# A rotary embedding kernel: an alignment instruction ahead of VectorE's and GpSimd's work

## The chip, the cores and the metric

The kernel runs on one core of a Trainium2 chip. The metric is the device time of one execution in microseconds (us). A profile of one execution is at hand as well: every instruction of the five engines (TensorE = PE, VectorE = DVE, ScalarE = ACT, GpSimd = POOL, SyncE = SP), and every packet that the core's 16 DMA engines moved, with its start, its duration, its size and its queue.

## The reference

The input `x` has 8 batches of 2048 positions, 8 heads and 64 numbers per head, in float32 (33.5 MB); `cos` and `sin` are tables of 2048 x 32. Each head's vector is split into two halves, which are rotated:

```python
x1 = x[..., : x.shape[-1] // 2]
x2 = x[..., x.shape[-1] // 2 :]
out1 = x1 * cos - x2 * sin
out2 = x1 * sin + x2 * cos
return np.concatenate([out1, out2], axis=-1)
```

The output is as large as `x`, so at least 67 MB have to pass between HBM and the core's memory.

## The kernel before, in words

The 2048 positions are laid over 128 partitions, 16 positions each, so that a batch is a tile `xt` of 128 x 8192 float32 (4 MB). Five such buffers turn (`NBUF = 5`): SyncE's queue loads batches 0 to 4 at once (L67; batch 0 in three parts, with the cosine table behind the first of them, L69), and later a batch whenever the buffer of the batch five before it has been stored. ScalarE's queue loads the sine table first (L76) and then stores the finished batches (L74); the last batch is stored in three parts by SyncE's queue. The results are written over `xt` in place.

A batch is rotated in four pieces of 128 x 2048 (batch 0 and the last batch have two half pieces each). For most of them, kind "A" in the code, GpSimd makes `t2`, the halves of x swapped and multiplied by sin and by -sin (L122, two instructions), VectorE makes `t1`, x times cos (L129), and VectorE adds the two into `xt` (L136). In five pieces the addition goes elsewhere: kinds "B" and "C" add in TensorE through an identity matrix (L143, L144, L160, L161), and ScalarE copies the sum from PSUM into `xt` (L145, L165); in kind "C" VectorE makes the sine product too (L148) and GpSimd has no part in it.

The order on each engine is the order in which the code writes the instructions (`keep`). Ahead of the loop over batches stand the preparations. GpSimd fills the identity matrix `eye` (L80, L81), ScalarE makes the table -sin, a copy of sin in PSUM and the negated identity (L90 to L92), and VectorE copies cos to PSUM (L93). GpSimd's first product waits for the sine table and the first part of x, VectorE's copy for the cosine table.

The whole program is straight-line code: VectorE goes through 115 instructions and GpSimd through 95, waiting instructions and the barriers at both ends included. These instructions are themselves brought to the engines by DMA: the profile lists packets of the kind "instruction" on a queue of their own, q14.

Of the kernel before, what the change touches and what calls it, by code (L numbers as in the profile page):

```python
# [10 lines left out]
def kernel(  # L11
# [7 lines left out]
    nc = tc.nc  # L19
    keep = tc.keep_in_program_order  # L20
# [30 lines left out]
    eye = const_pool.tile([P, P], f32, tag="eye")  # L51
# [25 lines left out]
    for b in range(NBUF):  # L77
        load(b)

    nc.gpsimd.memset(eye, 0.0)  # L80
    nc.gpsimd.affine_select(  # L81
        out=eye,
        in_=eye,
# [140 lines left out]
```

## Time and profile before

| | |
|---|---|
| time, three runs | 163.49, 163.62, 163.76 us; median 163.62 us |
| span of the profiled execution, first to last instruction | 161.8 us |
| what the median has over that span | 1.8 us |
| VectorE busy | 140.1 us, 87% of the span |
| GpSimd busy | 138.9 us, 86% |
| TensorE busy | 49.4 us, 31% |
| moved by the DMA engines | 67.65 MB, 418 GB/s over the span |
| packets of instructions within the span | 2, 0.02 MB |

For the profiled execution the page gives the span as its own time; what lies around it is known only as the 1.8 us by which the median of the runs is longer. "Busy" counts the time in which an engine executes an instruction. The profile's picture of the span cuts it into 40 slices of 4.0 us and gives a digit per slice, the busy share in tenths; its row DMA is the mean over the 16 DMA engines. A packet's record has start, duration, size and queue, but not the DMA engine that moved it. q1 is SyncE's queue, q10 ScalarE's.

### The profile page before, as it was taken

How to read it: one execution, taken by the hardware profiler on the slowest of the kernel's cores; microseconds unless marked ns; L12 is line 12 of the kernel's file. 1: busy time of each engine (PE TensorE's matmuls, PEld its weight loads, DVE VectorE, ACT ScalarE, POOL GpSimd, SP SyncE). 2: the span in 40 equal slices, each digit the busy share in tenths (PEclk: the TensorE clock that was granted, in tenths of full speed). 3: DMA queues.
4: the chain of work that ended last, by engine and by line, in shares of the span. 5: the costliest groups of instructions: out<-in, count | busy, mean ns of one | idle time of the engine just before them, and what ended most of it. 6: DMA issues, size and time to landing. Idle time of an engine off the chain costs nothing.

```text
span 161.8 us, 459 instructions
## 1 busy us (share of the span) xinstructions
PE 49.4 (31%) x80; PEld 18.5 (11%) x80; DVE 140.1 (87%) x66; ACT 12.8 (8%) x14; POOL 138.9 (86%) x70
## 2 busy tenths in 40 slices
PE   0000000597309760978049714972000000000000
PEld 0000000142004220322023301330000000000000
DVE  0297999999999999999999999199989999899950
ACT  3300000002200220021000220022000000000000
POOL 1399997998999999992999959999899997999800
PEclk9999999999975998589957995699655555555555
DMA  5999999999999999899899999999999999999995
GB/s 158 425 454 494 413 308 446 413 470 405 462 405 462 389 502 405 389 510 397 389 510 397 389 512 397 397 502 397 397 488 413 405 478 413 405 478 409 397 419 225
DMA packets 3314, 67.65 MB, mean 418 GB/s; under 512 B 368, under 2 KB 368, under 8 KB 624
## 3 DMA queue, kind: packets, MB, share of 16 engines
q1 hardware_dynamic: 2016, 38.01, 55.5%
q10 hardware_dynamic: 1296, 29.62, 42.6%
q14 instruction: 2, 0.02, 0.0%
HBM read 34.08 MB, written 33.55 MB: 418 GB/s over the span
## 4 chain that ended last, share of the span: by engine, by line
DMA 48%; DVE 37%; POOL 9%; issue 2%; DVEq 0%; SPq 0%; POOLq 0%; ACTq 0%
DMA xt<-in_x_dram 26%; DVE t L129 18%; DMA out_dram<-xt 18%; DVE xt L136 17%; POOL t L122 9%; DMA sin_sb<-in_sin_dram 4%; DVE t L148 1%; DVEq L136 0%; SPq L67 0%; POOLq L122 0%; ACTq L74 0%
## 5 line engine op out<-in xcount | busy, mean ns | idle before, releaser
L122 POOL TENSOR_TENSOR t<-xt,sin_sb 128x1024 f32<-128x1024 f32 (+1 forms) x32 | 70.4, 2199 | 13.5 <-DMA xt<-in_x_dram 8.3
L129 DVE TENSOR_TENSOR t<-xt,cos_ps 128x2048 f32<-128x2048 f32 (+1 forms) x34 | 73.4, 2167 | 0.8
L122 POOL TENSOR_TENSOR t<-xt,nsin 128x1024 f32<-128x1024 f32 (+1 forms) x32 | 70.3, 2196 | 0.0
L136 DVE TENSOR_TENSOR xt<-t,t 128x2048 f32<-128x2048 f32 (+1 forms) x29 | 62.2, 2145 | 8.2 <-POOL t L122 5.5
L143 PE MATMUL o<-t,eye 128*128 128x512 f32 x24 | 17.0, 799 | 23.1 <-DVE t L129 19.6
L160 PE MATMUL o<-t,eye 128*128 128x512 f32 x16 | 12.0, 844 | 37.8 <-DVE t L129 35.6
L144 PE MATMUL o<-t,eye 128*128 128x512 f32 x24 | 14.9, 709 | 0.0
L145 ACT COPY xt<-o 128x1024 f32<-128x1024 f32 x6 | 6.1, 1012 | 45.7 <-PE o L144 45.7
L143 PEld LDWEIGHTS o<-t,eye 128*128 128x128 f32 x24 | 5.5, 256 | 32.5 <-issue 26.5
L160 PEld LDWEIGHTS o<-t,eye 128*128 128x128 f32 x16 | 3.7, 256 | 43.2 <-issue 39.4
L165 ACT COPY xt<-o 128x1024 f32<-128x1024 f32 x4 | 4.0, 1012 | 47.8 <-PE o L161 47.8
L93 DVE COPY cos_ps<-cos_sb 128x512 f32<-128x512 f32 x1 | 0.7, 695 | 6.9 <-DMA cos_sb<-in_cos_dram 6.9
L144 PEld LDWEIGHTS o<-t,eye 128*128 128x128 f32 x24 | 5.6, 234 | 8.2 <-issue 7.6
L161 PE MATMUL o<-t,neye 128*128 128x512 f32 x8 | 6.3, 875 | 0.2
L148 DVE TENSOR_TENSOR t<-xt,sin_ps 128x2048 f32<-128x2048 f32 x2 | 4.6, 2281 | 0.0
L161 PE MATMUL o<-t,eye 128*128 128x512 f32 x8 | 4.1, 592 | 0.0
L161 PEld LDWEIGHTS o<-t,neye 128*128 128x128 f32 x8 | 2.2, 300 | 5.3 <-issue 3.6
L161 PEld LDWEIGHTS o<-t,eye 128*128 128x128 f32 x8 | 1.5, 190 | 1.9 <-issue 1.9
L90 ACT ACT_TABLE_LOAD x1 | 1.3, 1283 | 1.2 <-PEq L208 1.2
L90 ACT ACTIVATE nsin<-sin_sb 128x512 f32<-128x512 f32 x1 | 0.6, 629 | 4.0 <-DMA sin_sb<-in_sin_dram 4.0
L91 ACT COPY sin_ps<-sin_sb 128x512 f32<-128x512 f32 x1 | 0.6, 580 | 0.0
L80 POOL MEMSET eye<- 128x128 f32 x1 | 0.2, 204 | 0.3 <-POOLq L208 0.3
(6 smaller groups left out, 1.0 us busy)
## 6 DMA issues: line engine op xcount, KB each, us to landing
xt<-in_x_dram SPq DMA_DIRECT2D x7, 4096.0 KB, 42.8
out_dram<-xt ACTq DMA_DIRECT2D x6, 4096.0 KB, 27.2
out_dram<-xt ACTq DMA_DIRECT2D x2, 2048.0 KB, 22.3
xt<-in_x_dram SPq DMA_DIRECT2D x2, 1024.0 KB, 6.7
xt<-in_x_dram SPq DMA_DIRECT2D x1, 2048.0 KB, 12.2
out_dram<-xt SPq DMA_DIRECT2D x1, 2048.0 KB, 9.9
out_dram<-xt SPq DMA_DIRECT2D x2, 1024.0 KB, 6.2
sin_sb<-in_sin_dram ACTq DMA_DIRECT2D x1, 256.0 KB, 5.7
```

What stands on the lines that cost most here:

```text
L90: keep(nc.scalar.mul(nsin, sin_sb, -1.0))
L93: keep(nc.vector.tensor_copy(cos_ps, cos_sb))
L122: nc.gpsimd.tensor_mul(out=t2u[:, :, u, :].rearrange("p (r h) d -> p r h d", h=H), in0=xu[:, :, 1 - u, :].rearrange("p (r h) d -> p r h d" ...
L129: nc.vector.tensor_mul(out=t1.rearrange("p (r k d) -> p r k d", r=nr, d=Dh), in0=xk, in1=rep(cos_ps[:, r0 : r0 + nr, :], 2 * H),)
L136: keep(nc.vector.tensor_add(out=xt, in0=t1, in1=t2))
L143: nc.tensor.matmul(oc, eye, t1[:, cs], start=True, stop=False)
L144: nc.tensor.matmul(oc, eye, t2[:, cs], start=False, stop=True)
L145: keep(nc.scalar.copy(xt[:, 2 * j * C : 2 * (j + 1) * C], o))
L148: nc.vector.tensor_mul(out=t2.rearrange("p (r k d) -> p r k d", r=nr, d=Dh), in0=xk, in1=rep(sin_ps[:, r0 : r0 + nr, :], 2 * H),)
L160: nc.tensor.matmul(oc, eye, t1u[:, gs, u, :], start=True, stop=False)
L161: nc.tensor.matmul(oc, eye if u else neye, t2u[:, gs, 1 - u, :], start=False, stop=True)
L165: nc.scalar.copy(xu[:, :, u, :], o.rearrange("p (g d) -> p g d", d=Dh))
```

## The change

Behind the loads of the first five batches, each of the two engines gets one alignment instruction: first VectorE, then GpSimd. It makes the loader place the engine's next instruction at a multiple of 256 instructions in that engine's code. The slots that are skipped are filled up, and `max_nops=0` says that the engine doesn't run through the filling but branches over it. On VectorE the next instruction is the copy of the cosine table, and on GpSimd the clearing of `eye`. The clearing is now also kept in program order, behind the alignment.

```diff
     for b in range(NBUF):
         load(b)
 
-    nc.gpsimd.memset(eye, 0.0)
+    for eng in (nc.vector, nc.gpsimd):
+        keep(eng.addr_align(256, max_nops=0))
+    keep(nc.gpsimd.memset(eye, 0.0))
     nc.gpsimd.affine_select(
         out=eye,
         in_=eye,
```

Apart from the two added instructions, the order of the instructions and their waits on all five engines are the same in both programs. From the boundary to the program's end VectorE has 112 instructions and GpSimd 86.

## The prediction

> **What bounds the kernel now.** I read the busy times first, then the picture of the span, the chain that ended last, a table by stage, and last the DMA packets one by one. The page:
>
> ```profile
> PE 49.4 (31%) x80; PEld 18.5 (11%) x80; DVE 140.1 (87%) x66; ACT 12.8 (8%) x14; POOL 138.9 (86%) x70
> ...
> DMA  5999999999999999899899999999999999999995
> ...
> q1 hardware_dynamic: 2016, 38.01, 55.5%
> q10 hardware_dynamic: 1296, 29.62, 42.6%
> q14 instruction: 2, 0.02, 0.0%
> ...
> DMA 48%; DVE 37%; POOL 9%; issue 2%; DVEq 0%; SPq 0%; POOLq 0%; ACTq 0%
> ```
>
> No engine is busy throughout, but the 16 DMA engines are: 9 in every slice but the first, the last and one that says 8, and 55.5 + 42.6 = 98.1% of all their time. The table by stage (columns: PE, PE loads, DVE, ACT, POOL busy with counts, granted clock, DMA share, GB/s) says the same more sharply:
>
> ```profile
> 0.00:2.00 2.00, 0.00 (x0) 0.00 (x0) 0.00 (x0) 0.84 (x1) 0.70 (x6) 1.00 0.27 45
> 2.00:6.50 4.50, 0.00 (x0) 0.00 (x0) 0.00 (x0) 0.47 (x2) 0.00 (x0) 1.00 0.95 359
> 6.50:16.00 9.50, 0.00 (x0) 0.00 (x0) 7.90 (x6) 1.33 (x3) 9.47 (x7) 1.00 1.01 431
> 16.00:62.50 46.50, 20.05 (x32) 7.47 (x32) 45.44 (x21) 4.05 (x4) 44.84 (x20) 0.93 1.01 428
> 62.50:94.00 31.50, 19.55 (x32) 7.29 (x32) 30.84 (x14) 3.25 (x4) 28.50 (x13) 0.78 1.00 433
> 94.00:134.30 40.30, 9.76 (x16) 3.76 (x16) 35.44 (x17) 2.83 (x3) 36.81 (x17) 0.67 1.00 431
> 134.30:156.00 21.70, 0.00 (x0) 0.00 (x0) 20.48 (x11) 0.00 (x0) 18.60 (x10) 0.50 1.00 429
> ```
>
> From 6.5 to 156 us the share is 1.00: no DMA engine has a free moment. The end is therefore the time of the first packet (1.76 us) plus the work of the DMA engine that has most of it, and a VectorE or GpSimd that is a little later or earlier moves the end only if a queue runs dry by it. Next, what the two engines do at the start, where the change puts its jump:
>
> ```profile
> 0.73 0.20 POOL L80 MEMSET eye<- 128x128 f32 x1 [0.29 <-POOLq L208]
> 1.01 0.29 POOL L81 TENSOR_SCALAR_AFFINE_SELECT eye<-eye 128x128 f32<-128x128 f32 x1
> 6.53 1.26 POOL L122 TENSOR_TENSOR t<-xt,sin_sb 128x512 f32<-128x512 f32 x1 [5.23 <-DMA sin_sb<-in_sin_dram]
> 6.93 0.69 DVE L93 COPY cos_ps<-cos_sb 128x512 f32<-128x512 f32 x1 [6.93 <-DMA cos_sb<-in_cos_dram]
> ```
>
> Both stand idle until a table has landed: GpSimd for 5.23 us, VectorE from the barrier's end at 0.66 us for 6.2 us.
>
> The last view is the packets (start, end, queue, bytes, ns) around the two instruction packets and at the end:
>
> ```
> 94.392 -> 94.701 q14 8192 309       119.999 -> 120.308 q14 8192 309
> 94.703 -> 96.267 q10 32768 1564     120.305 -> 121.734 q1 32768 1429
> last packets of the 16 DMA engines end: 12 up to 160.02, one 160.09, then 160.33, 160.49, 160.55
> ```
>
> A 32768-byte packet takes 1213 ns in 1568 of 1664 cases. On the engine of the first fetch it would have run from 94.392 to 95.605; it ended at 96.267, 0.66 us later (309 ns of fetch, and the packet behind it 351 ns slow). The second fetch cost its engine 121.734 - 121.212 = 0.52 us. Nothing gives that back, as the engines never idle; and indeed 13 of the 16 engines end by 160.09 and three later. The last store lands at 160.91, the span ends 0.85 us after that in the closing barriers.
>
> Who fetches: at 94.39 us VectorE, and at 120.00 us GpSimd, are each at about the 69th of their instructions. I read that as each of the two engines passing a block boundary in its code there and asking for the next block. Neither is held up by it: VectorE's L136 starts 94.86 - 92.47 = 2.39 us after the L129 before it, as elsewhere (90.14 - 87.74 = 2.40), and GpSimd goes from 119.59 to 121.86, 2.27 us, as elsewhere.
>
> **The change part by part.**
>
> *The two alignment instructions and their branches.* They run right behind the opening barrier, at about 0.7 us. No row shows such a branch; the waiting and register instructions around it take 0.02 to 0.05 us. At the code jumped to, the block may have to be fetched. Bounds: nothing, and the 5.7 us from issue to landing of a 256 KB table, a far larger transfer; the nearest pair of rows is issue to first packet, 1.76 - 0.73 = 1.03 us, plus one 0.31 us packet: about 1.3 us, an estimate, which I take. GpSimd's `eye` then ends near 2.6 instead of 1.30 us, and the first product still waits for sin until 6.53; VectorE waits for cos until 6.93. Cost 0. If that cover of 5.2 and 6.2 us were gone, each 1 us of fetch would be 1 us of later products. Queued behind the jump is only the engines' own work; ScalarE's negated identity, which needs `eye`, runs at 7.53. SP's and ACT's queues hold every DMA and aren't touched, so the loads start at 1.76 as before.
>
> *`keep` on the memset.* It stands where it stood in the order: 0.
>
> *The two fetches at 94 and 120 us.* From the boundary VectorE has 112 instructions left and GpSimd 86. The Trainium skill (page "Runtime: NRT & Kernel Launch", section "What's in a NEFF") gives an instruction 64 bytes, by which a packet of 8192 holds 128 of them and both fit in one. With the next boundary behind the program's end, both fetches leave the saturated stage: their engines end 0.66 and 0.52 us sooner, at 159.8 to 160.0. The third late engine (160.33), which no fetch explains, then sets the end: 160.55 - 160.33 = 0.22 us gained. Bounds: 0, if the fetches stay, and 160.55 - 160.09 = 0.46 us, if the third engine's lateness goes too. I take 0.22.
>
> *The fetches at the start.* Two per engine: the block jumped to, and the one behind it. Each costs its DMA engine 0, if it runs before 1.76 us when all are idle, to 0.66 us, as at 94 us. Starting about 1 us after the jump they fall on the edge: the stage 2.0 to 6.5 us still has 5% x 4.5 = 0.22 us of idle time per engine. If they use the rings of the same two DMA engines, 2 x 0.31 - 0.22 = 0.4 us is added where 0.66 and 0.52 are taken away; those two engines end near 160.2 and 160.5 - 0.1 = 160.4 at worst, much like the third. I take nothing more than the third engine's end. Ends: 0, and 2 x 0.66 = 1.32 on one engine, less its 0.52 to 0.66: +0.7 us.
>
> **Sum** against the profiled execution: 161.8 - 0.2 + 0 = 161.6 us; with the 1.8 us around it, against the median of 163.62, 163.4 us.
>
> The Trainium skill speaks against any gain (same page, section "Instruction fetch mechanics"): passing a 16 KiB boundary is mostly hidden, while a taken branch out of the two blocks held makes the engine wait for a fetch. As to the engines the trace agrees (2.39 and 2.27 us, no gap); it shows 8 KiB packets, and the delay on the DMA engines that the page doesn't count. By that rule alone the sum would be 163.6, the branch being covered; no run here shows the branch yet.
>
> **The rivals.**
>
> 1. *The whole lateness goes.* Everything beyond the 13 punctual engines comes with the fetches, or the third engine's delay was the profile's own. For it: those three stand out only in the later part of the span. Against it: at the landings of 89.8 to 91.4 us, before any fetch, one engine was already some 0.15 us behind. End at 160.09: -0.46, 163.15 us; with -0.35 to -0.45, 163.2.
> 2. *The start takes more than the middle gives (slower).* Both blocks' packets come after 1.9 us, between the first loads, on one DMA engine: 0.66 us each. It decides from 0.33 us beyond what the middle gave back; +0.35 to +0.7: 164.0 to 164.3. For it: by my estimate the packets fall just there. Against it: the first packets of x take 0.8 to 1.0 us instead of 0.31, waiting rather than moving, and can let a fetch in between.
> 3. *The jump stalls beyond its cover (slower).* The fetch would have to last over 5.2 us on GpSimd or 6.2 us on VectorE; then the first products come late, and the last store, which follows the one before it without a gap and has about 0.5 us in hand (issue 156.05 + 1.03 against 157.56), comes late with them. A fetch of 8 us costs about 2: 165.6. Against it: 256 KB land in 5.7 us.
> 4. *Nothing moves.* The aligned code still passes a boundary inside the span, or the late engines are late for other reasons: 163.6.
>
> **How the numbers follow.** What a measurement of this kernel can tell from no change is about 0.2%, 0.33 us: under 163.29 is faster, over 163.95 slower. Forecast 0.42 and nothing moves 0.13, both within: 0.55. Rival 1: 0.27, faster. Rival 2: 0.13, rival 3: 0.05, slower, 0.18. The range takes in rival 1 with 0.05 for the runs' spread, 163.1, and goes up into rival 2, 164.0; what is left out is about 2 in 10. The forecast's own range is 163.3 to 163.6.
>
> **What would show it.** No instruction packet between 3 and 156 us; up to four in the first 3 us; no 1564 or 1429 ns packet at 94 and 120; the latest DMA engine ending near 160.3; GpSimd's first product still at 6.5 and VectorE's copy at 6.9. Instruction packets still in the middle speak for rival 4, three late engines with both packets at the start for rival 2, and a first product after 7 us for rival 3. I would be wrong altogether if the DMA engines ran dry somewhere, so that the products' timing counts.

## The result and the profile after

The changed kernel takes 164.45 us (median of five runs, 164.16 to 164.61) against 163.62: slower, ratio 1.005 with a 95% interval of 1.0039 to 1.006. That is +0.83 us, beyond the range of the prediction (163.1 to 164.0) and on the side of its second rival. The profiled execution took 164.60 us, its span 162.8, so that again 1.8 us lie around the span. In five of the kernels below some executions, one of twelve up to five of ten, took at least 2 us longer than the others (two of them 292 us), and they are left out of the ratios and of the ranges of times.

From the page of the changed kernel, the lines that answer to those shown of before:

```profile
span 162.8 us, 461 instructions
...
PE 49.5 (30%) x80; PEld 18.6 (11%) x80; DVE 140.1 (86%) x66; ACT 12.8 (8%) x14; POOL 138.9 (85%) x70
...
DMA  5999999999999999999999999999999999998983
...
q14 instruction: 4, 0.03, 0.1%
```

The engines do the same work in the same time (VectorE 140.1, GpSimd 138.9 us). What differs is the end of the DMA row (8, 9, 8, 3 where it was 9, 9, 9, 5) and the packets of instructions, four instead of two. The DMA view cut to the first 9 us, and to the stretch from 93 to 121 us in which the kernel before had its two:

```profile
q1 hardware_dynamic: 438, 2.54, 73.2%
q10 hardware_dynamic: 144, 0.26, 8.1%
q14 instruction: 4, 0.03, 1.5%
```

```profile
q10 hardware_dynamic: 205, 6.19, 51.2%
q1 hardware_dynamic: 213, 6.06, 50.2%
```

All four packets are in the first window, none is in the second: the aligned code passes no boundary in the middle any more. What the two engines do at the start, from the timeline:

```profile
3.47 0.20 POOL L82 MEMSET eye<- 128x128 f32 x1 [3.04 <-issue]
3.75 0.29 POOL L83 TENSOR_SCALAR_AFFINE_SELECT eye<-eye 128x128 f32<-128x128 f32 x1
6.73 1.27 POOL L124 TENSOR_TENSOR t<-xt,sin_sb 128x512 f32<-128x512 f32 x1 [2.69 <-DMA sin_sb<-in_sin_dram]
7.18 0.69 DVE L95 COPY cos_ps<-cos_sb 128x512 f32<-128x512 f32 x1 [7.18 <-DMA cos_sb<-in_cos_dram]
```

GpSimd's branch is recorded at 0.69 us, its next instruction at 3.47: the jump costs 2.8 us of waiting. It is covered, as the sine table is still on its way; the first product starts 0.2 us later than before (6.73 against 6.53) because the table lands 0.2 us later.

The loss sits in one DMA engine. Each transfer is split over the 16 DMA engines, and the trace has the time at which each of them finished its part. Seen from the median of the 16:

| transfer | before: median, slowest, lag | after: median, slowest, lag |
|---|---|---|
| third part of batch 0 | 9.28, 9.40, 0.12 us | 9.12, 10.57, 1.45 us |
| load of the last batch | 133.47, 134.32, 0.85 | 132.23, 135.22, 2.99 |
| last store | 160.29, 160.91, 0.62 | 160.72, 161.92, 1.20 |

From 10 us on one engine is some 1.4 us behind, and it stays behind (the 2.99 us hold one whole packet of 1.2 us more, by my reading because the two queues take turns; at the two landings ahead of the last store's the lag is 1.77). Its delay comes in these steps, by the packets (start, end, queue, bytes, ns). A packet's record doesn't name its DMA engine; that the steps fall on one is read from ends and starts that fit, and from the lags:

```
1.745 -> 2.780 q14 8192 1035     jump: the block jumped to
7.266 -> 7.591 q14 8192 325      the block behind it
7.579 -> 8.547 q1  8192 968      the packet that follows, 309 ns elsewhere
```

At the landing of the first loads this engine is some 0.5 us late; the second packet adds 0.33 and the slow one behind it 0.66 us, together 1.4 to 1.5. That the first 0.5 us come from the first packet isn't shown: in the four kernels without a packet of instructions at the start (the one before and three below) the slowest engine is 0.12 to 0.44 us late at the third part of batch 0 too. Then the delay goes through the kernel. The load of the last batch is complete when its slowest part is, 0.90 us later than before; so GpSimd and VectorE work through the last batch 0.9 us later, SyncE issues the last store at 156.96 instead of 156.05, and the punctual DMA engines run dry: their mean busy share is 0.55 from 157.0 to 157.5 us and 0.39 from there to 157.8, where both were about 1 before (0.97 and 1.04). The span doesn't hang on that gap. The late engine finishes its part of the store ahead only at 159.46, when the last store's packets have been coming since 157.79, so it always has data waiting; it finishes at 161.92 instead of 160.91: +1.01 us, the lengthening of the span.

### The profile page after: what moved, and what is told of

It reads as the page before. It is cut to its first block, busy times and chain, and to the rows that moved or that the text cites. A ratio compares the mean times of both kernels' runs of the same rounds, so it can differ in the third digit from the quotient of the medians.

```text
span 162.8 us, 461 instructions
## 1 busy us (share of the span) xinstructions
PE 49.5 (30%) x80; PEld 18.6 (11%) x80; DVE 140.1 (86%) x66; ACT 12.8 (8%) x14; POOL 138.9 (85%) x70
## 4 chain that ended last, share of the span: by engine, by line
DMA 68%; DVE 17%; POOL 8%; SPq 2%; issue 1%; DVEq 0%; POOLq 0%; ACTq 0%
DMA xt<-in_x_dram 50%; DMA out_dram<-xt 17%; DVE xt L138 10%; POOL t L124 8%; DVE t L131 7%; SPq L67 2%; SPq L69 0%; DVEq L138 0%; POOLq L124 0%; ACTq L74 0%
```

## The experiments

Three theories were on record. **D**: packets of instructions between the loads delay their DMA engine, and the slowest DMA engine sets the end. **C**: the products start later, and that sets the end. **I**: SyncE's third load, issued in 1287 ns instead of 424, is late by the 0.86 us that are lost.

**One engine alone.**

```diff
-    for eng in (nc.vector, nc.gpsimd):
+    for eng in (nc.vector,):
         keep(eng.addr_align(256, max_nops=0))
```

> Only VectorE gets the alignment to 256; GpSimd's code stays where it was. Theory D (late DMA engine): each packet of instructions that falls between the loads makes its DMA engine late, nothing gives that back, and the latest of the 16 sets the end. In the changed kernel the latest one took two of the four packets, at 1.74 us and at 7.27 us (0.4 and 1.0 us late), and I take both for VectorE's, as its copy starts at 7.18. Then this kernel has three packets, two before 8 us and GpSimd's at 120 us, the last landing is again about 1.2 us behind the median of the 16, and the time is 164.2 to 164.5. Rival C (late products): the products start later because of the jump, VectorE's copy at 7.2 instead of 6.9; then the loss is that 0.2 us: 163.8. Rival I (late issue): SyncE's third load was issued in 1287 ns instead of 424 and the 0.86 us go straight to the end; then the time follows that one issue, 164.4 where it is long and 163.6 where it is 424 ns.

Measured: 164.25 us, ratio 1.0034 (1.0021 to 1.0047). The packets came at 1.79, 6.83 and 120.89 us; at the third part of batch 0 the slowest DMA engine is 1.35 us behind the median, at the end 1.18. Theory D's numbers. The third load was issued in 908 ns, half of the way back to 424, and most of the loss is still there.

```diff
-    for eng in (nc.vector, nc.gpsimd):
+    for eng in (nc.gpsimd,):
         keep(eng.addr_align(256, max_nops=0))
```

> Only GpSimd gets the alignment to 256. Theory D: GpSimd's packets at 1.64 and 6.67 us made one DMA engine 0.7 and another 0.2 us late in the changed kernel; VectorE's packet at 94 us is back with its 0.66 us. So three DMA engines are 0.2 to 0.7 us late and none 1.4: the time is that of before within 0.2 us, 163.6 to 163.9. Rival C: GpSimd's first product starts at 6.7 instead of 6.5, so 163.8. Rival I: 164.4 if SyncE's third load takes 1287 ns to issue, 163.6 if 424. If the loss is there in full with one engine late by 1.2 us or more, I have given the packets to the wrong engine.

Measured: ratio 1.0016 (0.9999 to 1.0034); the runs lie in two groups, 163.5 to 164.0 and 164.3 to 164.8, which one profile can't tell apart. In the profiled execution (163.53 us) no DMA engine is more than 0.5 us behind at the third part of batch 0, and the last landing, 160.82, is that of before. Its first product starts at 6.73 us, exactly where it does in the changed kernel, which loses 0.83 us: theory C doesn't hold for those 0.2 us. Together with the kernel before this one, that points to VectorE's packets. For the second group, which is as slow as the changed kernel, there is no profile, and it may lose its time on GpSimd's packets.

**A jump into a block that is already there.**

```diff
-        keep(eng.addr_align(256, max_nops=0))
+        keep(eng.addr_align(128, max_nops=0))
```

> Both engines, but aligned to 128 instead of 256. If a packet of 8192 bytes is a block of 128 instructions and the next block is always held beforehand, the jump lands in code that is already there: no wait of 2.75 us on GpSimd, whose first instruction behind the jump starts near 0.8 us and not at 3.47, and only one packet per engine, for the block behind. No packet at 94 and 120 us, as 112 and 86 instructions fit into one block. Theory D: the two packets come near 1.7 us, when the DMA engines are just beginning, and cost 0.2 to 0.4 us each instead of 0.66 and 0.52 us in the middle: 163.3 to 163.6, faster than before by up to 0.3 us. If they come at about 7 us as in the changed kernel, they cost 0.6 to 1.0: 163.6 to 164.0. Rival C: the products start as before, 163.6. Rival I: the issue of the third load is 424 ns without fetches to collide with, 163.6.

Measured: ratio 1.0011 (1.0001 to 1.0021), no gain. The group of GpSimd's first instruction behind the jump:

```profile
L82 POOL MEMSET eye<- 128x128 f32 x1 | 0.2, 205 | 0.7 <-POOLq L210 0.7
```

It starts at 1.15 us; in the changed kernel it sat 3.0 us idle. One packet per engine is left (1.75 and 3.64 us), none in the middle, as forecast. But one of them still fell among the loads: one DMA engine is 0.9 us behind the median at the third part of batch 0, more than the 0.66 and 0.52 us that the middle gives back. Most of it is the packet at 3.64 (309 ns) and the data packet behind it, 8192 bytes in 841 ns instead of 309. That the kernel would be faster than before by up to 0.3 us didn't come true.

> Only GpSimd, aligned to 128. In the kernel with both engines at 128 the packets came at 1.75 us, which I take for VectorE's as it stood at 1.74 to 1.79 in each kernel in which VectorE jumps, and at 3.64 us, which would be GpSimd's; the first made one DMA engine 0.6 us late, the second none by more than 0.1. So here: one packet near 3.6 us that costs 0.1 us, none at 120 us, VectorE's at 94 us back with 0.66 us. Theory D: one or two late DMA engines instead of three, the time between 163.4 and 163.7. If the packet of GpSimd is the costly one, one engine is 0.6 us late from the first loads on and the time is 163.7 to 164.0. Rival I, by the issue of the third load, has already failed: it took 424 ns in the slowest kernel so far.

The same with GpSimd alone: ratio 0.9998 (0.9989 to 1.0008). Its packet came at 1.74 us, not at 3.6: I had exchanged the two engines. It costs next to nothing there (no DMA engine more than 0.4 us behind at the third part of batch 0), VectorE's is back at 94.51 us, and the sum is that of before.

> Only VectorE, aligned to 128. Theory D: one packet near 1.75 us that makes one DMA engine 0.5 to 0.6 us late from the first loads on, no packet at 94 us, GpSimd's at 120 us back with 0.52 us on another DMA engine: 163.6 to 164.0, like the kernel with both at 128. If late products (rival C) set the time, it follows the start of VectorE's copy: 6.9 as before gives 163.6, 7.6 as with both at 128 gives 164.3.

With VectorE alone: ratio 1.0023 (1.0012 to 1.0035), 163.8 to 164.2 us where 163.6 to 164.0 was expected; the packet came at 3.76 us, again the other way round than I had put it. One DMA engine is 1.0 us late at the third part of batch 0, where 0.5 to 0.6 was expected. Its copy starts at 7.77, for which theory C would have had about 164.4.

**The dose doubled.**

```diff
     keep(nc.gpsimd.memset(eye, 0.0))
+    keep(nc.gpsimd.addr_align(256, max_nops=0))
```

(with the first alignment on GpSimd alone)

> Only GpSimd, with a second alignment to 256 behind the clearing of eye, so that it jumps twice: the dose is doubled. The second jump costs another 2.75 us of waiting, from 3.7 to 6.5 us, and is just covered by the wait for the sine table. Theory D: two packets more than in the kernel with one jump on GpSimd, now while all DMA engines are busy, 0.3 to 1.0 us each; if they share a DMA engine with the earlier two, the last landing is 1.3 to 2 us behind the median and the time is 164.5 to 165.2; spread over other DMA engines, 163.8 to 164.3. Rival C: the products start at 6.7 to 7.0, so 163.8 to 164.0. Rival I: as the kernel with one jump, since the second jump comes after the issue of the third load.

Measured: 168.45 to 168.67 us in three executions and 166.44 in two, ratio 1.0246 (1.0197 to 1.0295), far more than expected, and I with a third load issued in 424 ns is out. The profiled execution is of the longer ones (168.64 us). The timeline shows why the step was too small:

```profile
3.67 0.20 POOL L82 MEMSET eye<- 128x128 f32 x1 [3.23 <-issue]
10.51 0.29 POOL L84 TENSOR_SCALAR_AFFINE_SELECT eye<-eye 128x128 f32<-128x128 f32 x1 [6.63 <-issue]
```

The second jump, made while the loads run, waited 6.6 us for its block, not 2.75. So the products are late as well, and dose and lateness are mixed. The packets came at 2.08, 7.66, 8.62, 13.88 (GpSimd's) and 98.96 us, and the slowest DMA engine ends 3.63 us behind the median. Not all of that is packets of instructions: with GpSimd's four through, at 16 us, the slowest engine is 2.13 us behind. From 73 to 111 us come 15 packets of ScalarE's queue that take over 1260 ns, 4.1 us more together than 15 of 1213 ns; most are spaced as on one DMA engine, and none follows a packet of instructions. So this run can't show what a dose costs. The next two take lateness and packets apart.

**The lateness alone.** The kernel before, with GpSimd held up ahead of its first product:

```diff
+    spare = t2_pool.tile([P, UNIT], f32, tag="t2")
+    for _ in range(5):
+        keep(nc.gpsimd.memset(spare, 0.0))
```

> The kernel before, without any alignment; GpSimd clears a spare tile of 128 x 2048 five times ahead of its first product. From the row of eye (204 ns for 128 columns, 98 ns for one column) I estimate 1.8 us for one, so that the first product starts near 10.3 us instead of 6.5. It has the lateness of the kernel in which GpSimd jumps twice (10.76), and no packet more. Theory D: the queues are full at that time, GpSimd gives the 3.8 us back in its waits for loads (8.3 us in the kernel before), and the end, which the DMA engines set, moves by 0 to 0.5 us: 163.6 to 164.2. Rival C (late products set the end): 3.8 us later, 167.4; in between, up to 2 us, would say that a part of what the kernel with two jumps lost was lateness.

Measured: 164.22 us, ratio 1.0032 (1.0022 to 1.0042). The first product starts at 10.47 us, as late as with two jumps, and the time is 4.4 us shorter in the profiled executions. The groups of GpSimd in this kernel and its waits in the kernel before show where the 3.9 us went:

```profile
L126 POOL TENSOR_TENSOR t<-xt,sin_sb 128x1024 f32<-128x1024 f32 (+1 forms) x32 | 70.6, 2208 | 3.1 <-DVE xt L140 2.7
L97 POOL MEMSET spare<- 128x2048 f32 x5 | 9.0, 1805 | 0.2
```

```profile
POOL t L122 <- DMA xt<-in_x_dram: 8.3, 6, 3.0
POOL t L122 <- DMA sin_sb<-in_sin_dram: 5.2, 1, 5.2
```

A late GpSimd no longer waits for loads at all (8.3 us in the kernel before): it gives the lateness back. 3.9 us late cost 0.55, at a lateness twenty times that of the changed kernel, and not even that is shown to be C's: in this execution 57 packets of 32768 bytes that follow no packet of instructions took over 1260 ns outside the stretch from 19 to 28 us, where the first stores begin, and in the kernel before none did.

**The packets alone.** The kernel before, with jumps on ScalarE where it has nothing to do:

```diff
                 store(b, *outs.pop(0))
+        if b in (2, 3):
+            keep(nc.scalar.addr_align(256, max_nops=0))
```

> The kernel before, and ScalarE gets an alignment to 256 behind its store of batch 2 (62.9 us) and another behind that of batch 3 (81.3 us). There ScalarE has nothing to do for 8 to 9 us, so a wait for the block jumped to, 6.6 us in the kernel with two jumps on GpSimd, is covered, and no product, load or store is issued later. What is added is the packets alone: two per jump, up to four, while all DMA engines are busy. Theory D: each costs its DMA engine 0.5 to 1.0 us. All on one engine, it ends 2 to 4 us late and the time is 165 to 167; spread over several, each 0.5 to 1 late like the two of before, 163.7 to 164.3; I take the first to be likelier, as in the kernel with two jumps one engine had all of it. Rivals C and I expect no change, 163.6, since nothing starts or is issued later.

Measured: 165.11 us, ratio 1.0095 (1.0082 to 1.0109). The DMA view from 60 to 95 us counts the four added packets and VectorE's at 94.64:

```profile
q1 hardware_dynamic: 268, 7.77, 51.6%
q10 hardware_dynamic: 257, 7.37, 48.9%
q14 instruction: 5, 0.04, 0.3%
```

and the packets, each followed on its DMA engine by a slow one of 32768 bytes (1213 ns elsewhere):

```
67.480 -> 67.789 q14 8192 309      67.786 -> 69.245 q1  32768 1459
74.088 -> 74.397 q14 8192 309      74.400 -> 75.859 q10 32768 1459
85.534 -> 85.843 q14 8192 309      85.840 -> 87.429 q1  32768 1589
91.054 -> 91.363 q14 8192 309      91.360 -> 92.953 q1  32768 1593
```

Each costs 309 ns and 246, 246, 376 and 380 ns of the packet behind it: 0.56 to 0.69 us, 2.48 us in all. At the last store the slowest DMA engine is 2.24 us behind the median, and the last landing is at 162.37 instead of 160.91, +1.46 us; the time is +1.44. That is less than 2.48, as before another engine set the end that was itself 0.62 us behind the median. No store or product starts late enough for that (the last store is issued at 156.27, 0.22 us after that of before). One load, the last, is issued 2.0 us later (93.52 instead of 91.50), as it waits for a store whose slowest part lands at 93.39; but it lands complete at 134.56, 0.24 us later than before. This is the disputed cost by itself, and it is theory D's. The first packet comes 4.8 us after the store ahead of the jump, the second 6.6 us after the first. I read that as a request for instructions standing in line behind the data; the next kernel bears on it.

**The loads out of the way.** The changed kernel, with the first loads waiting for GpSimd's jump:

```diff
+    for eng in (nc.vector, nc.gpsimd):
+        keep(eng.addr_align(256, max_nops=0))
+    keep(nc.gpsimd.memset(sin_sb[:, 0:1, 0:1], 0.0))
     keep(nc.scalar.dma_start(out=sin_sb, in_=sin_src))
...
         xt = xpool.tile([P, ROW], f32, tag="xt", name=f"xt{b}")
+        if b == 0:
+            keep(nc.gpsimd.memset(xt[:, 0:1], 0.0))
```

> The changed kernel (both engines at 256), but the first loads of SyncE's and ScalarE's queues wait for two small memsets that GpSimd does right behind its jump, so no load is under way while the four packets are fetched. Before: 161.8 us of span, first packet of data at 1.76 us, last landing at 160.91, so 159.15 us between them; in the changed kernel 161.92 - 1.73 = 160.2. Theory D: with nothing to wait behind, all four packets come between 1.6 and 4 us, before or just with the first data; no DMA engine is late, and from the first packet of data to the last landing it takes 158.7 to 159.2 us, at least 1.0 less than in the changed kernel. The wait itself moves the whole by about 2.5 us, so the time is 165.3 to 166.1. If something else than these packets costs the 0.8 us, the stretch stays near 160.2 and the time is 166.8 to 167.2. Rival C, that late products set the end: here they start 5 us behind the first data as always, so it too expects 159.2.

Measured: 166.29 us, ratio 1.0183 (1.016 to 1.0206). All four packets (1.65, 1.75, 3.91 and 4.41 us) start before the first data, ScalarE's at 4.48 and SyncE's at 4.66, as the DMA view of the first 4.5 us counts:

```profile
q14 instruction: 4, 0.03, 3.2%
q10 hardware_dynamic: 3, 0.01, 0.4%
```

From SyncE's first packet of data to the last landing it takes 163.54 - 4.66 = 158.9 us: 1.3 less than in the changed kernel (160.2) and 0.3 less than before (159.15). From ScalarE's first packet, the first of all here, it is 159.1: 1.1 and 0.1 less. The slowest DMA engine ends 0.58 us behind the median. The wait moved the whole by 2.9 us, 0.4 more than I had put, so the time is just above the expected 166.1.

> The control of the kernel before this one: the same two memsets and waits ahead of the first loads, and no alignment. The loads start some 0.3 us later than in the kernel before; the packets of instructions come at 94 and 120 us again, as 2 instructions more on GpSimd move its boundary by less than 3 us. Theory D: the stretch from the first packet of data to the last landing is that of before, 159.2, and longer than in the kernel with jumps and waits by 0 to 0.5 us; the time 163.8 to 164.2.

The control without alignment: 163.79 us, ratio 1.0008 (1.0 to 1.0017), the stretch 161.11 - 1.90 = 159.2 us. The gain that the prediction had looked for would be 0.1 to 0.3 us of DMA time here, by one profiled execution each. Executions of the kernel before lie between 163.42 and 164.21 us, so it isn't shown; and the wait costs 2.9. What is shown is that the 0.8 us of the changed kernel go when its fetches have no data to collide with. One of its packets came at 101.59 us, where I had expected less than 3 us of shift from 120; why was not followed up.

**All together.** Of each profiled execution, the packets of instructions within the span, the start of GpSimd's first product, the landing of the last store on the slowest DMA engine, and the time:

| kernel | packets at, us | first product | last landing | time | time less landing |
|---|---|---|---|---|---|
| changed | 1.6, 1.7, 6.7, 7.3 | 6.73 | 161.92 | 164.60 | 2.68 |
| VectorE only | 1.8, 6.8, 120.9 | 6.78 | 161.62 | 164.33 | 2.71 |
| GpSimd only | 1.6, 6.4, 94.2 | 6.73 | 160.82 | 163.53 | 2.71 |
| both at 128 | 1.8, 3.6 | 7.20 | 161.32 | 163.99 | 2.67 |
| GpSimd at 128 | 1.7, 94.5 | 6.67 | 161.08 | 163.78 | 2.70 |
| VectorE at 128 | 3.8, 120.9 | 7.36 | 161.54 | 164.22 | 2.68 |
| GpSimd twice | 2.1, 7.7, 8.6, 13.9, 99.0 | 10.76 | 165.93 | 168.64 | 2.71 |
| GpSimd late | 96.6, 99.2 | 10.47 | 161.53 | 164.24 | 2.71 |
| ScalarE jumps | 67.5, 74.1, 85.5, 91.1, 94.6, 120.7 | 6.69 | 162.37 | 165.05 | 2.68 |
| loads behind the jump | 1.6, 1.8, 3.9, 4.4 | 9.37 | 163.54 | 166.23 | 2.69 |
| loads wait only | 94.5, 101.6 | 6.74 | 161.11 | 163.79 | 2.68 |

The last column hardly changes: the time follows the landing on the slowest DMA engine in every one of them. It doesn't follow the first product: 6.73 us stands beside 163.53 and beside 164.60. None of them is faster than the kernel before.

## Why the prediction was wrong

- *What bounds the kernel*: right. The 16 DMA engines have no free time, and the one with the most work and delay sets the end. That VectorE and GpSimd are each at about their 69th instruction at the two fetches is rough: the profile has 64 rows of VectorE ahead of the one and 70 of GpSimd ahead of the other.
- *The alignment instructions and their branches*: cost 0 was right, by the cover of 5.2 us, not by the size. The wait was 2.8 us where 1.3 was estimated. That estimate took the first packet's way for the whole; the packet of GpSimd's block ended at 2.16 us and the engine went on at 3.47. The Trainium skill (page "Runtime: NRT & Kernel Launch", section "Instruction fetch mechanics") says that a taken branch out of the blocks held forces a fetch before the engine can go on; the trace agrees, 2.8 us at a jump to 256 and 0.4 us (eye at 1.15 instead of 0.73) at a jump to 128. The 16 KiB blocks it gives are packets of 8192 bytes here, and a jump to a boundary of 128 instructions finds its block there, as `eye` starts at 1.15 us and the first packet of instructions comes only at 1.74.
- *The two fetches at 94 and 120 us*: right that they go. The gain, put at 0.22 us, was not shown: with the loads out of the way the stretch is 0.1 to 0.3 us shorter than before, within the spread of the executions. In the changed kernel it would be lost under the next term.
- *The fetches at the start*: this is the step that failed. I set them at 0.4 us for a DMA engine with two packets, less than what the middle gives back, and so at nothing for the end. Measured, the slowest engine is 1.45 us behind the median once batch 0 has landed, 0.98 us of it from the second packet and the data packet behind it, and the last landing moved by +1.01 us. Three parts of the term were off. The 0.4 us count 0.31 us for each packet and leave out the slow data packet behind it, which the prediction itself had read as 0.35 us in the middle; behind the second packet it was 0.66. The idle time that I credited (0.22 us) could help only the first pair: the second pair came at 6.67 and 7.27 us, in the full stream, and so against the sign that no packet would come between 3 and 156 us. It came 5.0 and 5.5 us after the first pair; with the loads out of the way it came 2.3 and 2.7 us after it, so I read the rest as standing in line behind the loads. And the two packets of VectorE seem to have met on one DMA engine (1.35 us of lag with VectorE's jump alone), which I had allowed for only as the upper end (+0.7 us). With that end the sum would have been 164.1 to 164.3; the second rival, with a chance of 0.13, was the right mechanism, though only the second packets came after its 1.9 us, and still a little small.
- *What was not in the prediction*: a DMA engine that is late at the load of the last batch holds up the products of that batch, and with them the issue of the last store (+0.91 us), so that the punctual engines run dry near the end. The time doesn't hang on it here, as the late engine has data throughout.
- The fourth rival's "nothing moves", and the third's stall beyond its cover, didn't occur in the changed kernel; the stall did in the one in which GpSimd jumps twice, 6.6 us under load.

Not settled: the third late DMA engine of the kernel before, to which no packet of instructions belongs; why GpSimd's alignment alone gives two groups of times; where the slow data packets come from that follow no packet of instructions, with GpSimd jumping twice or starting late; and why VectorE's packet comes only at 3.7 us after a jump to 128, when GpSimd's comes at 1.74. Behind every instruction packet traced here in the full stream there is a slow data packet; why it is slow stays open.

## What to carry to other kernels

Where all DMA engines are busy from start to end, look at the slowest of the 16 and not at their mean: what makes one of them the last, by 0.6 us, say, is paid at the end, and packets of instructions can do so. The jump to an alignment didn't take fetches away here: at 256 it made four at the start out of two in the middle, at 128 two out of two. By this account it could help only if they fell where no data moves, and none of the kernels tried was faster. GpSimd, 85% busy, could start 3.9 us late for at most 0.55, so "what starts late" was the wrong place to look.

## What the runs showed of the hardware that I had not expected

- An instruction packet of 8192 bytes takes 309 ns on its DMA engine in the full stream, and the data packet behind it is slow by 0.21 to 0.53 us (32768 bytes; 8192 bytes: 0.26 to 0.66 us, the latter behind the one at 7.27): 0.5 to 1.0 us per packet.
- The wait for a block that isn't there is 2.5 to 3.0 us from the branch when few loads are under way and 6.6 us under full load (one kernel). ScalarE's four packets came all on one DMA engine, by its lag of 2.24 us at the end.
- Issuing its third load took SyncE 424 ns, or 554 to 1287 ns in kernels in which instructions were fetched near that moment. The time doesn't follow it: 803 ns with GpSimd at 128 (ratio 0.9998), 424 ns with GpSimd jumping twice (1.0246).
